# Split-weight blocks placed later, four more one-time slots for expert weights, in a fused transformer layer

## The chip, the cores and the metric

One core of a Trainium2 chip runs the whole layer as one program. The metric is the time of one execution on the device in microseconds (us). The engines named below are TensorE (PE; its weight loads are PEld), VectorE (DVE), ScalarE (ACT), GpSimd (POOL) and SyncE (SP), which here only issues transfers. Transfers are carried by 16 DMA engines shared by all queues.

## The reference

The layer takes 512 latent tokens and 256 context tokens of width 1024. It has two halves: token mixing (latent attention with 6 heads beside a Fourier mix of 256 channels, one output projection), and a mixture of 32 experts of which each token takes 4. The second half is the one that matters here:

```python
x = x + g1 * rms_norm(mix_x, norm_attn_post)           # after the output projection
hx2 = rms_norm(x, norm_ffn_pre) * (1 + sc2) + sh2
logits = hx2 @ w_router + b_router
top_logit, top_idx = lax.top_k(logits, 4)
gates = softmax(top_logit)
# for each expert e, over the tokens that chose it (xb):
g = minimum(xb @ w_gate[e] + b_gate[e], 7)
u = clip(xb @ w_up[e] + b_up[e], -7, 7)
y = (g * sigmoid(1.702 * g) * (u + 1)) @ w_down[e] + b_down[e]
# each token: the sum of its 4 y, weighted by its gates
x = x + g2 * rms_norm(moe, norm_ffn_post)
```

All is float32. Each of the 32 experts has three matrices of 1024 x 1024, 384 MiB in all, and every one of them has to be read.

## The kernel before

**The stages.** Up to about 335 us the kernel does the token mixing, ending with the output projection in four blocks of 128 tokens (`outp`). After each block follow `post(t)` (post-norm and residual on VectorE and ScalarE), `post_h(t)` (the token rows scaled by VectorE; for blocks 0 to 2 POOL adds the shift and stores the rows to `hx2_d` in DRAM; for block 3 VectorE adds), and `post_pe(t)` (router logits on PE, top 4 on VectorE). `pick(t)` gathers expert 0's tokens with matmuls. Then come the experts, to about 1335 us, and a short end with the last norm.

**The experts.** 32 units in a fixed order. Units 0 and 1 are experts 0 and 1, with 64 and 96 token slots; the others are chosen at run time by how many tokens came, and alternate: a larger one ("h", 128 slots, or "m", 96) and a smaller one ("l", 64, or "t", 32). Four are of kind "h"; their matmuls run on weights split into a high and a low part (`wsplit`: ScalarE writes the high part into `hi4`, VectorE the rest into `lo4`; four blocks of 4 KB per partition each, used in turn, 32 KB in all). The first "h" is unit 8, whose gate matrix is the 25th of 96 matrices (`order`).

**The weights.** A matrix comes in four pieces of 1 MiB (128 x 2 x 1024 float32), 384 pieces in the order of use. `load_piece(i)` issues piece i on SyncE's queue. Pieces 0 to NX - 1 go into one-time slots that are freed after use; the others share a ring of NRING = 11 slots. `emit_mat` computes one matrix; when it has used up piece p, it issues p + 11 if p is in the ring (p >= NX), otherwise it only frees the slot. `more_ring` takes the NX + NRING = 16 slots one after the other as memory of the first half comes free, and issues the piece that goes into each.

**A unit's tokens.** For each unit from 1 on, `gather` (inside `fetch_of`) computes row numbers, and POOL issues an indirect DMA (L1319) that reads the unit's token rows from `hx2_d`; `x_trans` transposes them on PE (the `tr` helper, L270) and copies them out of PSUM. `finish(ready.get(u))` puts all of that before the unit's first matmul.

**What sets the order.** Before the experts, a scheduler orders instructions by priority within what the data allow. From `manual_schedule` on (the expert phase) each engine runs in the order in which the code is written; `later` and `tick` delay single operations by a step. Memory is handed out by a list: PLAN holds one address per allocation, in the order of allocations. An allocation whose address overlaps an older block waits until that block's last use.

Helpers record most operations, so lines repeat: L266 matmul, L270 transpose, L274 ScalarE's activation, L278 two-input operation on VectorE or POOL, L289 VectorE's scalar-tensor-tensor, L978 the issue of a weight piece, L1144 and L1152 `post_h`'s product and shift.

Of the kernel before, what the change touches and what calls it, by code (L numbers as in the profile page):

```python
# [20 lines left out]
try:  # L21
# [6 lines left out]
F32R = mybir.dt.float32r  # L28
# [8 lines left out]
D = 1024  # L37
# [43 lines left out]
]  # L81


# [79 lines left out]
def dit_block(ctx: ExitStack, tc: tile.TileContext, x, c, cctx, c_ctx, w_mod, b_mod, n_ap, n_ao, n_fp, n_fo,  # L163
# [8 lines left out]
    vec_d = dr.tile([4, D], F32, name="vec_d")  # L172

    NRING = 11
    NX = 5
    WB = 5
    WT = 1
    WN = {2: 4, 3: 4, 4: 4, 5: 4}
    NB, LA = 4, 3
# [7 lines left out]
    def A(*dims, dt=F32, top=False):  # L187
        serial[0] += 1
        return T(nc, ar, f"s{serial[0]}", dims, dt, top)
# [14 lines left out]
    def alias(block, *dims, dt=F32):  # L204

        z = nc.alloc_sbuf_tensor_at(f"a{len(also)}", [128, *dims], dt, offset=block.o).ap()
        also[z.tensor.name] = block.t.tensor.name
        return z
# [48 lines left out]
    def free(*blocks):  # L257
        for z in blocks:
            n = z.t.tensor.name
            if any(n == q[0] for _, lo_, li_, _f in late for q in lo_ + li_):  # L260
                settle()
            z.free()
# [226 lines left out]
    for g in range(4):  # L489
        h = 64 * (g % 2)  # L490
# [454 lines left out]
    units = [("l", 0, None), ("m", 1, None)]  # L945
# [5 lines left out]
    order = [(0, "g"), (0, "u"), (1, "g"), (0, "d"), (1, "u"), (2, "g"), (1, "d")]  # L951
# [11 lines left out]
    def load_piece(i):  # L963
# [9 lines left out]
        else:  # L973
            src = wsrc[m][e:e + 1]
        slot = ring[i] if i < NX else ring[NX + (i - NX) % NRING]
        where[u, m, h] = slot
# [3 lines left out]
    def more_ring(n=None):  # L980
        while len(ring) < NRING + NX and (n is None or n > 0):
            ring.append(A(2, D))
            load_piece(len(ring) - 1)
            n = None if n is None else n - 1

    steps = [(u, m, k) for u, m in order for k in range(8)]

    def chunk(s):
        u, m, k = steps[s]
        return where[u, m, k // 2].f[:, k % 2]  # L990
# [191 lines left out]
    hi4, lo4 = [], []  # L1182

    def emit_split(s):
        if s < len(steps) and units[steps[s][0]][0] == "h":
            wsplit(s, chunk(s))

    def wsplit(s, z):
        hi, lo = hi4[s % NB].r, lo4[s % NB].r
        act(hi, z, AF.Copy)  # L1190
        later(lambda: tt(lo, z, hi, op=OP.subtract), [lo], [z, hi], age=0)

    for s in range(NB):
        hi4.append(A(D, dt=F32R))
        lo4.append(A(D, dt=F32R))
    for s in range(LA):
        emit_split(s)
    eid, eidi, selb = A(NS), A(NS, dt=I32), A(NS + 3, dt=BF)
    pm = CRp("pmod")
    V.memset(selb.b[:, NS + 2:NS + 3], 0.0)  # L1200
# [45 lines left out]
    kinds = [z[0] for z in units]  # L1246
# [198 lines left out]
    bank = {(0, "g"): 0, (0, "u"): 2, (1, "g"): 4, (0, "d"): 0, (1, "u"): 2, (2, "g"): 0, (1, "d"): 2}  # L1445
# [183 lines left out]
    def sel_of(u):  # L1629
        kind, e, r = units[u]  # L1630
        j = r if e is None else NS + e
        return selb.b[0:96, j:j + 1]
# [15 lines left out]
    def add(g, front=False):  # L1648
        z = Task(g)
        side.insert(0 if front else len(side), z)  # L1650
        return z
# [15 lines left out]
    def source(u, mat):  # L1667
        k = kinds[u]
        if mat == "d":
            return (aTh, aTl) if k == "h" else aTm if k == "m" else aT0 if u == 0 else aTf.f  # L1670
        return xT0 if k == "h" else (xT1.f if u == 1 else xTm) if k == "m" else xT64 if u == 0 else xTf.f
# [5 lines left out]
    def emit_mat(i, also=()):  # L1677
        also = list(also)
        for s in range(8 * i, 8 * i + 8):
            u, m, k = steps[s]  # L1680
            emit_split(s + LA)
            step_mm(kinds[u], m, bank[u, m], k, chunk(s), hi4[s % NB], lo4[s % NB], sel_of(u), source(u, m), u == 0)
            if k % 2:
                if s // 2 < NX:
                    free(ring[s // 2])
                elif s // 2 + NRING < len(pieces):
                    load_piece(s // 2 + NRING)
                else:
                    where[u, m, k // 2].free()
            side_step()  # L1690
            tick()
# [7 lines left out]
        yield  # L1699

    xT0 = (xTh, xTl)
    xTm = alias(xTh, 8, 128)
    ready, acted, summed = {}, {}, None
    add(routing())
    for i, (u, m) in enumerate(order):
        kind = kinds[u]
        if i:
            pu, was = order[i - 1]
            pk, pb = kinds[pu], bank[pu, was]
            if was == "g":  # L1710
                add(glu_g(pk, pb, pu == 0), True)
            elif was == "u":
                acted[pu] = add(chain(glu_u(pk, pb, {"h": 2, "m": 2, "l": 3, "t": 5}[kind] if pk == "h" else 0, pu == 0), a_trans(pk, pu == 0)), True)
            else:
                finish(summed)
                y_out(pu, pk, pb)
                if pu == 1:
                    summed = add(chain(chain_back(pu), rest(7), scatter(pu)))
                elif pu and pk in "lt":
                    summed = add(chain(chain_back(pu - 1), chain_back(pu), scatter(pu - 1, pu)))  # L1720
        if i == 5:
            summed = add(chain(bdown(), chain_back(0), scatter(0)))
        if i == 1:
            ready[1] = add(x_of(1))
        elif i == 2:
            add(fetch_of(2))
            add(fetch_of(0))
            add(fetch_of(3))
        elif i == 3:
            ready[2] = add(chain(x_of(2), fetch_of(4)))  # L1730
            add(chunk_plan())
        elif i == 6:
            ready[3] = add(chain(x_of(3), fetch_of(5)))
        elif m == "d" and u >= 2 and u + 2 < NU:
            x_ = x_of(u + 2)
            ready[u + 2] = add(chain(x_, fetch_of(u + 4)) if u + 4 < NU else x_)
        if (u, m) == (NU - 4, "g"):
            ntot, jcnt = W(1, dt=I32), W(1)
            cp(ntot.i, incl.f[:, NE - 1:NE])
            V.memset(jcnt.f, 0.0)  # L1740
            n_over = nc.values_load(ntot.i[0:1, 0:1], min_val=0, max_val=48, skip_runtime_bounds_check_because=SKIP)
        if m == "g":
            finish(ready.get(u))
        elif m == "d":
            finish(acted.get(u))
        if i + 1 == len(order):
            break
        emit_mat(i)
        if i == 0:
            settle()  # L1750
            t1, u1 = W(D), W(D)
            xT1 = W(8, 128)
        elif i == 1:
            while side:
                finish(side.pop(0))
            queued.close()
            free(lg, mask, maskb, Ub, onesb)
            aTh, aTl = R(8, 128), R(8, 128)
            aTm = alias(aTh, 8, 96)
            aT0 = alias(aTh, 8, 64)  # L1760
            yh, yl = R(D), R(D)
            acc = [W(D) for _ in range(4)]

            bdr = acc[3]
            for r in range(3):
                nc.sync.dma_start(bdr.f[32 * r:32 * r + 32], b_d)
        elif i == 4:
            settle()
            free(xT1)
            bd, gT, g3 = R(D), R(512), W(4, 96)  # L1770
            xTf = W(4, 128)
        elif i == 6:
            while side and side[0] is not ready[3]:
                finish(side.pop(0))
            settle()
            free(bd, g3, gT)
            aTf, u1l, yz = W(8, 64), W(512), R(D)
# [47 lines left out]
    for t in range(6):  # L1825
        if t < 4:
            for j in (2 * t, 2 * t + 1):
                both(j, j == 7, True)
            for j in (2 * t, 2 * t + 1):
                z = acc[t].f[:, 512 * (j % 2):512 * (j % 2) + 512]  # L1830
# [10 lines left out]
    with tc.For_i(0, n_over, 1):  # L1841
# [29 lines left out]
        for m in "gud":  # L1871
# [3 lines left out]
            for k in range(8):  # L1875
# [3 lines left out]
                z = slot.f[:, k % 2]  # L1879
# [37 lines left out]
```

## Time and profile before

| what | value |
|---|---|
| median of 3 runs | 1366.96 us (1366.21 to 1369.84) |
| the profiled execution, its own time | 1370.38 us |
| its span, first to last instruction | 1368.6 us |
| mean granted clock of TensorE | 0.986 |
| busy: PE, PEld | 1300.6 us (95%), 816.2 us (60%) |
| busy: VectorE, ScalarE, POOL | 740.0, 388.2, 119.3 us |
| moved by the DMA | 469.05 MB |

The profile is of one execution; its time is 1.8 us more than its span; differences are worked out from it and then carried to the median. Times in the trace count from the span's start. The busy share of an engine is a mean over the stages; which of two nearly full resources sets the end is to be read from who waits for whom.

### The profile page before, as it was taken

Reading aid. Unit: us, or ns where it says so; the run is one execution under the profiler, and the core shown is the slowest. Engines: PE = TensorE matmul, PEld = TensorE weight load, DVE = VectorE, ACT = ScalarE, POOL = GpSimd, SP = SyncE. Lnnn points to the kernel's source line nnn. Section 1 sums busy time; section 2 is a strip of 40 time slices with the busy share of each in tenths; the row PEclk is TensorE's granted clock in tenths of the full one; section 3 lists DMA queues with packets and bytes.
Section 4 is the critical chain, followed back from the end, with each engine's and each line's share of the span. In section 5 each row is a group of like instructions: output and inputs, shape, how many; then the busy total and the mean of one; then the engine's idle time right before and its main releaser. Section 6 shows DMA issues by size and latency. Waiting matters only on the chain. (4 is left out here: it accounts for less than half of the span.)

```text
span 1368.6 us, 33586 instructions
## 1 busy us (share of the span) xinstructions
PE 1300.6 (95%) x14518; PEld 816.2 (60%) x14518; DVE 740.0 (54%) x1393; ACT 388.2 (28%) x591; POOL 119.3 (9%) x89
## 2 busy tenths in 40 slices
PE   5999999999999999999999999999999999999993
PEld 3766888787455455566555555655555575555562
DVE  4676777756554334387343427752433477343675
ACT  5565444732111101054010103510110143010352
POOL 3355000003000000000000000000000000000002
PEclk8999999999999999999999999999999999999996
DMA  9876002749999999999999999999999999999993
GB/s 340 315 242 204 2 0 66 243 169 363 336 351 407 408 406 405 405 409 408 408 408 405 408 403 408 409 408 408 403 408 404 408 408 407 400 407 401 408 384 128
DMA packets 126507, 469.05 MB, mean 343 GB/s; under 512 B 10976, under 2 KB 12316, under 8 KB 126356
## 3 DMA queue, kind: packets, MB, share of 16 engines
q1 hardware_dynamic: 121540, 454.44, 84.9%
q0 software_dynamic: 4816, 12.43, 2.5%
q8 instruction: 115, 1.88, 0.6%
q14 instruction: 36, 0.29, 0.1%
HBM read 464.05 MB, written 6.31 MB: 344 GB/s over the span
## 5 line engine op out<-in xcount | busy, mean ns | idle before, releaser
L266 PE MATMUL ps<-s,s 128*32 128x256 f32 (+9 forms) x7307 | 874.0, 385 | 28.1 <-DVE s L278 10.0
L266 PEld LDWEIGHTS ps<-s,s 128*32 128x32 f32 (+3 forms) x6945 | 543.0, 139 | 297.2 <-issue 104.6
L266 PE MATMUL ps<-s,a 128*32 128x256 f32 (+1 forms) x6744 | 400.6, 384 | 0.0
L266 PEld LDWEIGHTS ps<-s,a 128*32 128x32 f32 x6744 | 212.2, 110 | 156.1 <-issue 20.6
L274 ACT ACTIVATE s<-s 128x1024 fp32r<-128x1024 f32 (+8 forms) x196 | 175.7, 926 | 388.6 <-DVE s L283 301.9
L278 DVE TENSOR_TENSOR s<-s,s 128x1024 fp32r<-128x1024 f32 (+11 forms) x316 | 207.9, 684 | 38.4 <-ACT s L274 34.7
L274 ACT ACTIVATE s<-ps 128x512 fp32r<-128x512 f32 (+5 forms) x151 | 82.6, 557 | 279.2 <-PE ps L266 139.2
L278 DVE TENSOR_TENSOR s<-s,ps 128x512 f32<-128x512 f32 (+1 forms) x129 | 86.2, 682 | 81.0 <-PE ps L266 80.5
L285 DVE TENSOR_SCALAR s<-ps 128x768 f32<-128x768 f32 (+3 forms) x32 | 26.1, 815 | 150.2 <-PE ps L266 150.2
L1319 POOL DMA_INDIRECT s<-hx_d,s x31 | 32.3, 1043 | 850.3 <-PE ps L266 577.6
L270 PE MATMUL ps<-s,s 128*128 128x128 f32 (+1 forms) x447 | 73.3, 286 | 18.0 <-DVE s L283 9.8
L293 DVE COPY s<-ps 128x4 f32<-128x4 f32 (+5 forms) x65 | 22.9, 358 | 123.3 <-PE ps L266 100.5
L270 PEld LDWEIGHTS ps<-s,s 128*128 128x128 f32 (+1 forms) x447 | 52.5, 144 | 54.0 <-issue 18.4
L289 DVE SCALAR_TENSOR_TENSOR s<-ps,s,s 64x512 fp32r<-64x512 f32 (+5 forms) x65 | 46.6, 718 | 54.9 <-ACT s L274 49.2
L274 ACT ACTIVATE s<-ps,s 64x512 fp32r<-64x512 f32 (+7 forms) x69 | 45.2, 665 | 93.5 <-PE ps L266 88.3
L297 DVE TENSOR_TENSOR s<-ps,s 128x512 fp32r<-128x512 f32 (+1 forms) x92 | 60.6, 667 | 19.1 <-ACT s L274 19.0
L283 DVE TENSOR_SCALAR s<-ps 128x768 f32<-128x768 f32 (+4 forms) x33 | 26.2, 795 | 75.4 <-PE ps L266 75.4
L278 POOL TENSOR_TENSOR s<-s,s 128x1024 f32<-128x1024 f32 (+1 forms) x19 | 43.3, 2288 | 251.6 <-DVE s L278 211.7
L274 ACT ACTIVATE a<-ps 128x512 f32<-128x512 f32 x22 | 13.1, 597 | 148.9 <-PE ps L270 148.8
L274 ACT ACTIVATE s<-s,s 128x1 f32<-128x1 f32 (+4 forms) x69 | 42.7, 646 | 13.2 <-DVE s L289 8.0
L297 DVE TENSOR_TENSOR s<-s,s 128x192 fp32r<-128x192 f32 (+5 forms) x32 | 36.0, 1144 | 8.8 <-ACT s L274 8.5
L289 DVE SCALAR_TENSOR_TENSOR s<-s,s,s 128x512 fp32r<-128x512 f32 (+5 forms) x47 | 36.4, 802 | 5.1 <-ACT s L274 4.6
(81 smaller groups left out, 327.5 us busy)
## 6 DMA issues: line engine op xcount, KB each, us to landing
s<-in_w_gate_dram SPq DMA_DIRECT2D x128, 1024.0 KB, 16.9
s<-in_w_up_dram SPq DMA_DIRECT2D x128, 1024.0 KB, 12.8
s<-in_w_down_dram SPq DMA_DIRECT2D x128, 1024.0 KB, 17.2
s<-in_w_mod_dram SPq DMA_DIRECT2D x32, 512.0 KB, 4.8
s<-in_w_mod_dram SPq DMA_DIRECT2D x8, 1024.0 KB, 13.5
s<-in_x_dram SPq DMA_DIRECT2D x8, 512.0 KB, 5.3
s<-in_w_out_dram SPq DMA_DIRECT2D x8, 512.0 KB
s<-in_w_in_dram SPq DMA_DIRECT2D x1, 2560.0 KB
```

Of the source, the lines that this page charges most:

```text
L266: pin(nc.tensor.matmul(o, a, b, start=start, stop=stop))
L270: pin(nc.tensor.transpose(o, i, ident))
L274: return nc.scalar.activation(o, i, f, **kw)
L278: return eng.tensor_tensor(o, a, b, op=op)
L283: eng.tensor_scalar(o, a, s1, s2, op0=op0)
L285: eng.tensor_scalar(o, a, s1, s2, op0=op0, op1=op1)
L289: V.scalar_tensor_tensor(o, a, s, b, op0=op0, op1=op1)
L293: eng.tensor_copy(o, i)
L297: later(lambda: eng.tensor_tensor(lo, src, hi, op=OP.subtract), [lo], [src, hi])
L1319: nc.gpsimd.indirect_dma_start(out=xg[kind], out_offset=None, in_=src, in_offset=bass.IndirectOffsetOnAxis(ap=idxs.i[:, u:u + 1], axis=0), ...
```

## The change

NX goes from 5 to 9: nine one-time slots, so 20 pieces instead of 16 have a place before the expert phase. The memory comes from the eight blocks `hi4` and `lo4`, which are no longer taken before the expert phase but right before the matrix ahead of the first "h" unit (while `emit_mat(23)` is about to run). Until then `emit_split` does nothing, and `step_mm` gets None in place of the blocks. PLAN has new addresses for nearly all allocations from there on, and the early ones of the expert phase with it. The ring keeps its 11 slots.

```diff
-    105120, 154272, 217088, 211456, 141984, 117408, 133792, 137888, 228288, 211328, 229088, 72096, 24736, 63776,
...
+    141984, 105120, 215552, 133792, 211456, 154272, 137888, 125600, 28896, 208416, 229088, 209728, 24736, 191264,
...
     NRING = 11
-    NX = 5
+    NX = 9
...
     def emit_split(s):
-        if s < len(steps) and units[steps[s][0]][0] == "h":
+        if s < len(steps) and units[steps[s][0]][0] == "h" and hi4:
             wsplit(s, chunk(s))
...
-    for s in range(NB):
-        hi4.append(A(D, dt=F32R))
-        lo4.append(A(D, dt=F32R))
-    for s in range(LA):
-        emit_split(s)
...
-            step_mm(kinds[u], m, bank[u, m], k, chunk(s), hi4[s % NB], lo4[s % NB], sel_of(u), source(u, m), u == 0)
+            step_mm(kinds[u], m, bank[u, m], k, chunk(s), *(z[s % NB] if z else None for z in (hi4, lo4)), sel_of(u), source(u, m), u == 0)
...
+    first_h = kinds.index("h")
...
+        if order[i + 1:i + 2] == [(first_h, "g")]:
+
+            for _ in range(NB):
+                hi4.append(A(D, dt=F32R))
+                lo4.append(A(D, dt=F32R))
         emit_mat(i)
```

SyncE's queue around the start of the expert phase stood so before (L1254 loads token numbers, L1766 expert biases; the w_down rows end expert 0, the w_up rows are expert 1's pieces 16 to 19; the last row reads an expert's number):

```order
L978 DMA s194_2585<-in_w_down_dram 128x2x1024
L978 DMA s208_2711<-in_w_down_dram 128x2x1024
L978 DMA s209_2713<-in_w_down_dram 128x2x1024
L978 DMA s212_2726<-in_w_down_dram 128x2x1024
L1254 DMA s222_2739<-in_tokens_dram 128x512
L978 DMA s181_2343<-in_w_up_dram 128x2x1024
L978 DMA s188_2537<-in_w_up_dram 128x2x1024
L978 DMA s189_2545<-in_w_up_dram 128x2x1024
L1766 DMA s250_2968<-in_b_down_dram 32x1024 x3
L978 DMA s190_2553<-in_w_up_dram 128x2x1024
L970 TENSOR_LOAD s204_2596
```

In the changed kernel the same stretch of the same queue is:

```order
L978 DMA s194_2585<-in_w_down_dram 128x2x1024
L978 DMA s200_2703<-in_w_down_dram 128x2x1024
L978 DMA s201_2705<-in_w_down_dram 128x2x1024
L978 DMA s204_2718<-in_w_down_dram 128x2x1024
L978 DMA s205_2720<-in_w_up_dram 128x2x1024
L978 DMA s206_2722<-in_w_up_dram 128x2x1024
L978 DMA s207_2724<-in_w_up_dram 128x2x1024
L978 DMA s208_2726<-in_w_up_dram 128x2x1024
L1249 DMA s218_2739<-in_tokens_dram 128x512
L1767 DMA s246_2965<-in_b_down_dram 32x1024 x3
L970 TENSOR_LOAD s196_2588
```

The four w_up pieces went into slots s181 and s188 to s190, used before; now they have slots of their own (s205 to s208) and stand directly behind the w_down pieces. Behind the last row both queues go on alike.

On VectorE the change shows in the last block of the output projection, between `post_pe(2)` (the first two rows) and `post(3)` (the last two); s161_2307 and s162_2308 are the token rows of blocks 0 and 1:

```order
 L289 SCALAR_TENSOR_TENSOR s176_2335<-ps_60,s186_2349 128x32
 L285 TENSOR_SCALAR s177_2336<-s158_2142,s176_2335,s170_2320 128x64
-L1144 SCALAR_TENSOR_TENSOR s207_2602<-s162_2308,s170_2320,s156_2136 128x1024
+L1144 SCALAR_TENSOR_TENSOR s199_2594<-s162_2308,s170_2320,s156_2136 128x1024
+L1144 SCALAR_TENSOR_TENSOR s198_2593<-s161_2307,s170_2320,s156_2136 128x1024
 L278 TENSOR_TENSOR s166_2312<-ps_60,s154_2134 128x512
 L285 TENSOR_SCALAR s170_2320<-s170_2320 128x1
```

Block 0's product stood one block earlier, before `post(2)`; it now stands behind block 1's, ahead of `post(3)`, since its output lies where the last output-projection weight (`woh[5]`) lay. POOL's add and store of block 0 move with it. From the first expert matmul on, the orders of PE, ScalarE and VectorE are the same in both.

## Rows read from the trace of the kernel before

**Rows 1.** The page: GB/s in 40 equal slices of the span (34.2 us each).

```profile
GB/s 340 315 242 204 2 0 66 243 169 363 336 351 407 408 406 405 405 409 408 408 408 405 408 403 408 409 408 408 403 408 404 408 408 407 400 407 401 408 384 128
```

**Rows 2.** Stretches: sum, busy PE, PEld, DVE, ACT, POOL (instructions), clock, DMA share, GB/s.

```profile
346.00:352.00 6.00, 4.81 (x76) 2.62 (x72) 3.24 (x11) 2.34 (x4) 0.00 (x0) 1.00 0.64 227
394.00:410.00 16.00, 16.00 (x209) 8.77 (x209) 8.98 (x17) 1.11 (x2) 0.00 (x0) 1.00 0.79 289
410.00:420.00 10.00, 10.00 (x188) 6.09 (x184) 3.12 (x10) 2.05 (x4) 1.00 (x1) 1.00 1.02 400
560.00:1320.00 760.00, 750.04 (x9215) 438.70 (x9211) 381.71 (x694) 166.65 (x223) 23.27 (x22) 1.00 1.03 407
```

**Rows 3.** Landing of weight pieces (L978) issued at 414:418, at 1085:1089, at 1317:1320.

```profile
DMA to landing us min/median/max: 6.2/7.0/7.8
DMA to landing us min/median/max: 20.0/20.1/20.2
DMA to landing us min/median/max: 18.7/19.4/20.1
```

**Rows 4.** PE's waits, 414 to 1320: total us, times, longest.

```profile
PE ps L266 <- DVE s L278: 8.9, 11, 1.8
...
```

**Rows 5.** ScalarE near the end: start, us, operation [idle before <-releaser].

```profile
1321.87 1.06 ACT L274 ACTIVATE s<-s 128x1024 fp32r<-128x1024 f32 x1 [8.27 <-DMA s<-in_w_down_dram]
```

**Rows 6.** SyncE's queue by time: start, us from first to last issue, operation, count.

```profile
347.54 6.49 SPq L978 DMA_DIRECT2D s<-in_w_up_dram  x3
...
356.58 0.39 SPq L978 DMA_DIRECT2D s<-in_w_up_dram  x1
...
394.24 23.38 SPq L978 DMA_DIRECT2D s<-in_w_up_dram  x8
```

**Rows 7.** PE's waits, 335 to 410, the whole answer.

```profile
PE ps L270 <- DMA s<-hx_d,s: 2.3, 2, 1.2
PE ps L270 <- DVE s L293: 0.6, 1, 0.6
```

**Rows 8.** PE by time: transposes of block 2, first expert matmuls, two gathers' transposes.

```profile
311.65 1.09 PE L270 MATMUL ps<-s,s 128*128 128x128 f32 x8 [0.77 <-DVE s L289]
...
335.69 6.25 PE L266 MATMUL ps<-s,a 128*32 128x256 f32 x112
...
348.66 0.63 PE L270 MATMUL ps<-s,s 128*128 128x128 f32 x4 [1.19 <-DMA s<-hx_d,s]
...
371.24 0.66 PE L270 MATMUL ps<-s,s 128*128 128x128 f32 x4 [1.15 <-DMA s<-hx_d,s]
```

**Rows 9.** Landing of gathers (L1319) issued at 340:350, 360:366, 410:420, 1086:1088.

```profile
DMA to landing us min/median/max: 4.5/4.5/4.5
DMA to landing us min/median/max: 8.8/8.8/8.8
DMA to landing us min/median/max: 5.1/5.1/5.1
DMA to landing us min/median/max: 7.4/7.4/7.4
```

**Rows 10.** POOL by time: two of its adds, and the gather of unit 1.

```profile
308.12 2.39 POOL L1152 TENSOR_TENSOR s<-s,s 128x1024 f32<-128x1024 f32 x1 [12.57 <-DVE s L1144]
...
320.53 2.35 POOL L1152 TENSOR_TENSOR s<-s,s 128x1024 f32<-128x1024 f32 x1 [7.87 <-DVE s L1144]
...
343.99 1.09 POOL L1319 DMA_INDIRECT s<-hx_d,s  x1 [4.41 <-issue]
```

**Rows 11.** VectorE by time, 306 to 324.

```profile
306.75 1.28 DVE L1144 SCALAR_TENSOR_TENSOR s<-s,s,s 128x1024 f32<-128x1024 f32 x1 [1.09 <-PE ps L266]
...
309.27 2.32 DVE L289 SCALAR_TENSOR_TENSOR s<-s,s,s 128x1024 f32<-128x1024 f32 x1
...
319.16 1.28 DVE L1144 SCALAR_TENSOR_TENSOR s<-s,s,s 128x1024 f32<-128x1024 f32 x1 [1.18 <-PE ps L266]
...
321.81 2.28 DVE L289 SCALAR_TENSOR_TENSOR s<-s,s,s 128x512 f32<-128x512 f32 x2
```

16 rows, old and new, of the table PLAN are left out of this document.

## The prediction

> **What bounds the kernel now.** I read four views in this order. The page first: of its 40 slices, the 13th (from 410 us) to the 38th all move 400 to 409 GB/s, those before it clearly less [rows 1].
>
> The table by stretch comes second. From 560 to 1320 us the DMA share is 1.03 at 407 GB/s and PE is busy 750.04 of 760 us, so both stand near their limit and no average tells which sets the end; from 410 to 420 the DMA is just as full (400 GB/s); but from 394 to 410 it carries only 289 GB/s while PE is busy all 16 us [rows 2]. So the saturated run begins at about 410 us.
>
> Third, who waits. From 414 to 1320 us the largest wait of PE is 8.9 us, for VectorE, and none of its rows names a weight transfer [rows 4]. What a loaded transfer shows instead is a growing queue: a weight piece issued at 414 to 418 lands after 7.0 us, at 1085 after 20.1, at 1317 after 19.4 [rows 3]. PE's releases thus come a little faster than the DMA can serve them, and only at the end is the eleven-piece cushion spent: ScalarE's split of the last 128-slot down-projection idles 8.27 us for a piece of w_down [rows 5]. The end is the start of the saturated run plus its bytes at 407 GB/s plus the tail. A change pays if it starts that run earlier, not if it takes a microsecond off PE after 420.
>
> Fourth, what starts the run. SyncE issues eight pieces over 23.38 us from 394.24 on [rows 6]: each goes out when PE has used up the piece eleven places before it, so in that stretch the DMA idles because PE has not yet freed a slot. PE's pace from its first expert matmul at 335.69 to about 410 is what starts the run, and from 335 to 410 nearly all that it waits for is two gathers of token rows, 2.3 us together, and no weights [rows 7]: 1.19 us before 348.66, 1.15 before 371.24 [rows 8].
>
> **The change part by part.**
>
> *Four more one-time slots.* Pieces 16 to 19 (expert 1's up-projection) lose their wait for the slots of pieces 5 to 8. Before, they are issued from 347.54 on, the last at 356.58 [rows 6]; now they have slots of their own, and they should go out at about 336, when the last attention blocks are freed. That is 4 x 1.049 MB / 407 GB/s = 10.3 us of transfer taken forward. But the ring is still eleven deep: piece 20 still follows the use of piece 9, and so on for all later ones. Since PE waits for no weights there [rows 7], these releases do not move, the DMA merely idles 10.3 us longer somewhere before 410, and the saturated run starts when it did. I cost this at 0. It needs the idle room of the stretch 394 to 410, where (407 - 289) / 407 x 16 = 4.6 us of transfer time lie empty before the full run; with that cover gone, the head start would be kept, as in the first rival.
>
> *Gather of expert 1, now beside full DMA.* POOL issues it at 343.99 [rows 10]; it lands in 4.5 us [rows 9], while the DMA moves 227 GB/s just after (346 to 352) [rows 2]. With pieces 16 to 19 in flight from 336 on, the pieces 12 to 19 keep the engines full until about 355, so this gather runs under load. Loaded gathers: 7.4 us at 1086, 8.8 at 360 to 366, 5.1 at 410 to 420 [rows 9]. PE already waits 1.19 us for it, so all that it grows is added to PE: 5.1 - 4.5 = +0.6 at least, 8.8 - 4.5 = +4.3 at most. I take the steady 7.4: +2.9. This shift lies ahead of 410, delays every release after it, and so the whole saturated run.
>
> The Trainium skill (DMA: Bandwidth & Descriptors, "Queues, rings and completion order") says that an engine takes turns between the queues that have work, a packet each. By that, a gather beside one full weight queue at most doubles, 4.5 to 9.0, and the sum below would be 4.5 - 2.9 = 1.6 us higher, an estimate; the trace agrees that a gather does not stand behind the whole backlog, since at 1086 it takes 7.4 us where weights take 20.1 [rows 3, 9].
>
> *Gather of expert 2.* It takes 8.8 us and costs PE 1.15 [rows 8, 9]. Now pieces 16 to 19 are out of its way, and only pieces 20 and on stand beside it. Anything at or under 7.4 takes the whole wait away (8.8 - 7.4 = 1.4, more than 1.15): -1.15, bounds 0 and -1.15.
>
> *Block 0's modulation moved.* hx[0] now lies where the last out-projection weight lay, so its multiply on VectorE, 1.28 us at 306.75 [rows 11], and POOL's add and store behind it, come after that of block 1, at the head of the last post-norm. Where it stood, it goes: at 309.27 an operation of the same shape takes 2.32 instead of 1.28 beside POOL's add (308.12, 2.39 us), and PE idles 0.77 before 311.65 for the line of that operation [rows 8, 10, 11]. Where it now stands, VectorE works from 319.16 on without a pause that could take it [rows 11], and the router of the last block hangs on it: +1.28. Net 1.28 - 0.77 = +0.5. POOL's adds slide too: now two stand in this chain. At 321.81 two operations of 128x512 take 2.28 us beside the add of 320.53 [rows 10, 11]. If POOL's add gets out of their way, about 1.1 us comes back (-0.6 in all); if the 0.77 isn't regained, +1.3. I take +0.5.
>
> *The rest.* The eight split blocks are placed before piece 92 is used instead of before the expert phase; no instruction is in that. The two engine orders from 336 on are the same on PE, ScalarE and VectorE. SyncE issues pieces 16 to 19 ahead of the small loads of token numbers and b_down; these are needed many us later: 0.
>
> Sum, against the profiled execution: 1370.38 + 0.5 + 2.9 - 1.15 = 1372.6. That execution is 3.4 us over the median of the runs shown, 1366.96, so the median of the changed kernel should be 1366.96 + 2.25 = 1369.2. Its own range, from the bounds: -0.6 + 0.6 - 1.15 = -1.15 to 1.3 + 4.3 - 0 = +5.6, 1365.8 to 1372.6.
>
> **Rivals.**
>
> *The head start is kept (faster).* If the DMA were in truth the limit from 336 on, 10.3 us of transfer moved forward would end the run 10.3 us sooner: 1366.96 - 10.3 = 1356.7. For it: the end waits for transfers [rows 5]. Against: 289 GB/s at 394 to 410 [rows 2], releases by PE [rows 6], and no wait of PE for weights before 410 [rows 7]. 0.09.
>
> *Gather 1 isn't slowed.* If weights and gather share the engines so that its few rows pass, only the second wait goes: 0.5 - 1.15 = -0.65, 1366.3. For it: 5.1 us at 410 to 420 under 400 GB/s [rows 2, 9]. Against: 7.4 and 8.8 elsewhere. 0.19.
>
> *Block 0's work lands whole in the last chain (slower).* VectorE's 1.28 and POOL's add of 2.35, which holds back VectorE's operations with two inputs as at 309.27 and 321.81 [rows 10, 11], both before the router, with nothing regained: 3.6 + 2.9 - 1.15 = +5.4, 1372.3. It decides if the first expert matmul, now at 335.69 [rows 8], starts at 339 or later. For it: VectorE has no pause there. Against: the 0.77 that goes, and VectorE's first operation may get ahead of POOL's add. 0.17.
>
> The Trainium skill (SBUF — State Buffer, "Who interferes with whom") has a rule that speaks for this rival: an operation of VectorE with two inputs in SBUF contends with a GpSimd instruction that reads SBUF, and whichever comes second is held back wholly. The 2.32 against 1.28 agrees.
>
> **How the numbers follow.** The forecast has 0.55, the rivals 0.09, 0.19 and 0.17. A measurement of this kernel tells a difference of about 0.3%, 4.1 us: "same" is 1362.9 to 1371.1. Of the forecast 0.07 lies above that (gather at 8.8 with the upper bound of the moved work), 0.48 in it; the second rival lies in it whole, of the third 0.02; the first is faster, with 0.01 more for a mixture. Faster 0.10, same 0.68, slower 0.22. The range: down to 1364.0, the second rival with its lower bounds (-0.6 - 1.15 = -1.75, 1365.2) and some 1.2 for the runs, of which the fastest lies 0.75 under the median; up to 1373.0, the third rival and 0.7 of the same. That leaves out the first rival and a few hundredths above.
>
> **What would show it.** In the changed trace: SyncE issues of w_up at about 336 instead of 347.5 (the head start); a hole in the DMA at about 355 to 360, and 394 to 410 again under 300 GB/s; weight pieces at 1317 again landing after 19 to 20 us; the gather issued at about 344.5 landing after 7 us, with PE waiting about 4 us for it; no wait at the second gather; the first expert matmul at about 336.2. The prediction is wrong if the saturated run starts more than 3 us earlier than 410, or if the queue at 1317 is clearly shorter with the last split's wait gone.

## The result, and the profile after

The changed kernel takes 1378.74 us (median of 6 runs, 1376.22 to 1381.25), the kernel before 1368.51 beside it (6 runs); the ratio is 1.0060, 95% interval 1.0041 to 1.0078. The medians themselves differ by 10.2 us (0.75%); the ratios here and below are those on record, which are not quotients of the two medians. Forecast were 1369.2, within 1364.0 to 1373.0: the time lies above the range, and the change is slower by 0.6%, not the same. The profiled execution took 1380.88 us with a span of 1379.1, so it is 10.5 us longer than the profiled one of before.

PE by time (start, us, operation, idle before it and what ended it), the changed kernel (the first line shown are the transposes of block 1, ahead of all that follows here):

```profile
297.95 0.60 PE L270 MATMUL ps<-s,s 128*128 128x128 f32 x4
...
322.89 0.66 PE L270 MATMUL ps<-s,s 128*128 128x128 f32 x4 [1.18 <-DVE s L289]
326.12 0.66 PE L270 MATMUL ps<-s,s 128*128 128x128 f32 x4 [2.57 <-DVE s L289]
326.61 9.49 PE L266 MATMUL ps<-s,s 128*128 128x64 f32 x48
...
342.03 6.25 PE L266 MATMUL ps<-s,a 128*32 128x256 f32 x112
...
360.62 1.12 PE L270 MATMUL ps<-s,s 128*128 128x128 f32 x4 [6.82 <-DMA s<-hx_d,s]
...
367.42 8.95 PE L266 MATMUL ps<-s,s 96*32 96x512 bf16 x156
```

The same view of the kernel before, the lines of it that were not shown:

```profile
298.50 0.60 PE L270 MATMUL ps<-s,s 128*128 128x128 f32 x4
...
324.64 5.47 PE L266 MATMUL ps<-s,s 128*128 128x64 f32 x48
...
353.42 11.55 PE L266 MATMUL ps<-s,s 96*32 96x512 bf16 x204
```

The first expert matmul starts 6.3 us later (335.69 in [rows 8]), and the transposes of unit 1's tokens wait 6.82 us for their gather instead of 1.19. The 0.77 us at 311.65 and the wait at the second gather are gone. Start times of two profiles hold an offset from earlier stages: block 1's transposes stand at 298.50 before and at 297.95 here, and in a second profile of the same changed kernel (c_after_again below) at 295.86. Counted from these transposes the first expert matmul comes after 37.2 us before and 44.1 us here, 6.9 later. Behind the wait for the gather, the work up to the next line shown takes 6.8 us (360.62 to 367.42) where it took 4.8 (348.66 to 353.42). The 48 matmuls behind the last block's transposes take 9.49 us instead of 5.47; the table by stretch says why (sum, busy PE, PEld, DVE, ACT, POOL, then clock, DMA share, GB/s):

```profile
328.00:336.00 8.00, 8.00 (x38) 8.00 (x40) 3.79 (x10) 0.00 (x0) 3.81 (x2) 0.50 1.02 410
354.00:358.00 4.00, 0.00 (x0) 0.00 (x0) 1.74 (x3) 0.00 (x0) 0.00 (x0) 1.00 1.01 286
358.00:374.00 16.00, 13.38 (x196) 7.35 (x200) 4.55 (x14) 1.20 (x2) 0.00 (x0) 0.79 0.06 14
410.00:420.00 10.00, 10.00 (x124) 5.29 (x127) 6.42 (x14) 0.82 (x2) 0.00 (x0) 1.00 0.67 229
560.00:1320.00 760.00, 750.90 (x9394) 438.52 (x9385) 373.25 (x686) 161.86 (x219) 23.29 (x22) 1.00 1.02 408
```

Behind each of the two idle stretches of PE the granted clock is at the lower of its two levels (0.50, which is 1.2 GHz, from 328 to 336; 0.79 as a mean of 358 to 374). In the kernel before it is 1.00 in every stretch shown [rows 2], and in the one of the 48 matmuls too:

```profile
328.00:336.00 8.00, 7.31 (x62) 5.32 (x65) 5.62 (x14) 0.81 (x2) 4.04 (x3) 1.00 0.90 357
```

And the DMA moves 14 GB/s from 358 to 374: the head start was spent in idling, as forecast. The lightly loaded stretch that lay at 394 to 410 lies behind 410 now (229 GB/s from 410 to 420). From 560 on both kernels run alike.

VectorE by time, in the changed kernel, at the place to which block 0's work moved:

```profile
317.59 2.48 DVE L1144 SCALAR_TENSOR_TENSOR s<-s,s,s 128x1024 f32<-128x1024 f32 x2 [1.86 <-PE ps L266]
...
321.44 4.62 DVE L289 SCALAR_TENSOR_TENSOR s<-s,s,s 128x512 f32<-128x512 f32 x2
```

POOL by time around it, up to the gather of unit 1:

```profile
318.96 3.32 POOL L1152 TENSOR_TENSOR s<-s,s 128x1024 f32<-128x1024 f32 x1 [0.33 <-DVE s L1144]
...
323.15 2.35 POOL L1152 TENSOR_TENSOR s<-s,s 128x1024 f32<-128x1024 f32 x1
...
341.24 0.52 POOL L1261 MEMSET s<- 128x512 f32 x1 [8.03 <-DMA hx_d<-s]
341.74 0.55 POOL L1155 DMA_DIRECT2D hx_d<-s  x1
350.77 1.09 POOL L1314 DMA_INDIRECT s<-hx_d,s  x1 [8.48 <-DVE s L278]
```

VectorE's pair of operations takes 4.62 us against 2.28 [rows 11]; the 2.34 more are the length of POOL's add of block 0 (2.35), which stands between them. PE waits for exactly these (2.57 at 326.12). The rule of the Trainium skill (SBUF — State Buffer, "Who interferes with whom") that the later of the two is held back wholly agrees with that.

The last three lines were not foreseen. The store of block 3's rows stands on POOL behind a memset of a gather buffer, and that memset waits until a store of hx_d has landed, since the buffer now lies where block 2's rows lay. The gather needs all four stores. In this profile the order costs little: VectorE's add of block 3 ends at 340.10, 1.6 us ahead of the store, and the gather goes out 8.7 us behind the first expert matmul, where it was 8.3 before (343.99 behind 335.69). What grew is its landing. Landing of the store issued at 341.74:

```profile
DMA to landing us min/median/max: 8.2/8.2/8.2
```

Landing of the gather issued at 350.77:

```profile
DMA to landing us min/median/max: 9.8/9.8/9.8
```

The gather took 4.5 before [rows 9]; block 3's store, issued at 334.29 in the kernel before, took 3.8:

```profile
DMA to landing us min/median/max: 3.8/3.8/3.8
```

SyncE's queue shows the head start (pieces 16 to 19 at 341, forecast at about 336) and that later releases moved with PE: the eight pieces issued from 394.24 on [rows 6] are 12.8 us later.

```profile
341.10 2.30 SPq L978 DMA_DIRECT2D s<-in_w_up_dram  x4
...
407.05 23.33 SPq L978 DMA_DIRECT2D s<-in_w_up_dram  x8
```

### The profile page after: what moved, and what is told of

It is laid out like the page before. It is cut to its first block, busy times and chain, and to the rows that moved or that the text cites. A ratio compares the mean times of both kernels' runs of the same rounds, so it can differ in the third digit from the quotient of the medians.

```text
span 1379.1 us, 33583 instructions
## 1 busy us (share of the span) xinstructions
PE 1306.9 (95%) x14516; PEld 822.0 (60%) x14518; DVE 739.6 (54%) x1393; ACT 388.2 (28%) x591; POOL 120.3 (9%) x89
## 5 line engine op out<-in xcount | busy, mean ns | idle before, releaser
L274 ACT ACTIVATE s<-s,s 128x1 f32<-128x1 f32 (+4 forms) x69 | 42.7, 647 | 12.7 <-DVE s L289 8.0
```

The source lines that it names most:

```text
L274: return nc.scalar.activation(o, i, f, **kw)
```

## The experiments

Twelve runs were made in three groups (the first four rows, the next four, the last four), each on one chip beside the kernel before; ratios of different groups come from different chips. Added lines shift the line numbers of the views a little. Two expectations call the gather's landing in the changed kernel 10.5 us; that was misread, it is the 9.8 above.

| run | edit, on the changed kernel | median us (n) | before beside it | ratio, 95% interval |
|---|---|---|---|---|
| e1_hx0_place | block 0's rows elsewhere | 1374.42 (12) | 1369.53 | 1.0038, 1.0023 to 1.0052 |
| e2_late_pieces | pieces 16 to 19 written later in the code | 1378.35 (6) | 1369.53 | 1.0060, 1.0038 to 1.0083 |
| e3_both_undone | both of these | 1375.09 (12) | 1369.53 | 1.0041, 1.0029 to 1.0054 |
| e5_keep_clock | PE kept busy in its wait | 1378.10 (6) | 1369.53 | 1.0060, 1.0037 to 1.0083 |
| e6_store_order | e1 and store ahead of memset | 1370.23 (12) | 1370.65 | 1.0011, 0.9995 to 1.0027 |
| e7_late_13_19 | e6 and pieces 13 to 19 held back | 1366.63 (12) | 1370.65 | 0.9975, 0.9964 to 0.9986 |
| e8_late_16_19 | e6 and pieces 16 to 19 held back | 1366.29 (12) | 1370.65 | 0.9968, 0.9951 to 0.9985 |
| e9_deeper_ring | e7 and three more ring slots at first | 1367.62 (12) | 1370.65 | 0.9989, 0.9972 to 1.0007 |
| c_after_again | none | 1379.67 (6) | 1370.45 | 1.0077, 1.0057 to 1.0097 |
| e5b_keep_clock | as e5 | 1376.98 (6) | 1370.45 | 1.0055, 1.0035 to 1.0075 |
| e10_store_order_only | store ahead of memset | 1380.00 (6) | 1370.45 | 1.0072, 1.0050 to 1.0094 |
| e11_late_16_19_only | pieces 16 to 19 held back | 1376.56 (12) | 1370.45 | 1.0037, 1.0019 to 1.0055 |

**e1_hx0_place.** The address of hx[0] alone:

```diff
-... 227264, 227392, 227680, 129696, 150176, ...
+... 227264, 227392, 227680, 221696, 150176, ...
```

> The changed kernel with one address altered: block 0's token rows (hx[0]) lie where no out-projection weight is still in use, so that VectorE's product and POOL's add of block 0 stand again before post(2). The four early pieces 16 to 19 stay early. Theory 1 (two separate causes: the moved add of POOL holds up VectorE and with it PE, whose clock then falls, +6.3 us up to the first expert matmul; and the gather of unit 1 beside full DMA, another 6 to 7 us): first expert matmul back at 335.7 +- 0.7 us instead of 342.0, no stretch at half clock before it, the gather still landing after 8 to 10.5 us with PE waiting 4 to 7 us; median 1371 to 1374, about 6 us under the changed kernel. Theory 2 (the early pieces alone do it, by loading the DMA; the moved add is harmless): no change, 1378 to 1379. Theory 3 (other new addresses are at fault): first expert matmul stays near 342.

PE by time in e1:

```profile
295.60 0.60 PE L270 MATMUL ps<-s,s 128*128 128x128 f32 x4
...
334.30 6.25 PE L266 MATMUL ps<-s,a 128*32 128x256 f32 x112
...
353.72 1.12 PE L270 MATMUL ps<-s,s 128*128 128x128 f32 x4 [7.65 <-DMA s<-hx_d,s]
```

The first expert matmul came at 334.30, 38.7 us behind block 1's transposes, against 44.1 in the changed kernel and 37.2 before: block 0's place explains 5.4 of the 6.9 us, part of them through the clock (looked at below). The other 1.5 us are as much as the 48 matmuls lose to a lower clock that stayed: they take 6.93 us instead of 5.47. The median fell by 0.2% in ratio, a little less than expected; PE now waits longer for the gather (7.65 us). POOL's lines show that the store of block 3 still stood behind the memset, though its add had begun at 330.91 and takes 1.22:

```profile
335.03 0.52 POOL L1261 MEMSET s<- 128x512 f32 x1 [7.08 <-DVE a L1226]
335.54 0.54 POOL L1155 DMA_DIRECT2D hx_d<-s  x1
344.99 1.10 POOL L1314 DMA_INDIRECT s<-hx_d,s  x1 [8.90 <-DVE s L1380]
```

Theory 2 fell. Of theory 1 the first half holds, but for its clock; the second half, a gather late only by full DMA, was incomplete: here, where block 3's add ends at 332.13, the memset holds its store until 335.54, and the gather goes out 10.7 us behind the first expert matmul.

**e2_late_pieces, e3_both_undone.** The same edit of the loading, on the changed kernel and on e1:

```diff
             ring.append(A(2, D))
-            load_piece(len(ring) - 1)
+            if len(ring) <= 16:
+                load_piece(len(ring) - 1)
...
                     free(ring[s // 2])
+                    if s // 2 >= 5:
+                        load_piece(s // 2 + NRING)
```

> The changed kernel, with pieces 16 to 19 in their own slots but issued only when PE has used up pieces 5 to 8, as in the kernel before; block 0's work stays moved. Theory 1: first expert matmul still near 342.0, the gather of unit 1 lands after 4.5 to 5 us and PE waits 1 to 1.7 us for it, the second gather costs about 1.2 again; PE is then some 6.3 us behind the kernel before and the median is 1373 to 1375. Theory 2 (early pieces alone): 1368.5, as before. If the head start were worth anything, this kernel would lose more than the changed one, over 1379.

> Both edits together: block 0's rows at a free address and pieces 16 to 19 issued as late as before, on the changed kernel's memory (nine one-time slots, split blocks taken late). Theory 1: the whole loss is gone, 1368.5 +- 2, first expert matmul at 335.7, gather of unit 1 landing after 4.5 us. Theory 3 (some other part of the change, as the new addresses or the late split blocks, costs too): over 1371.

Both missed: 1.0060 and 1.0041, no change against their bases. The edit did not do what was meant. Its place in the code puts a piece behind PE's step only if something makes SyncE wait, and a slot that nobody used makes it wait for nothing. In e3 pieces 16 to 18 go out from 332.71 on, before PE's first expert matmul at 333.64. So these two say nothing on the head start; what they showed is PE's wait in e3, 9.96 us, with the memset and store in the order above.

```profile
332.71 1.92 SPq L978 DMA_DIRECT2D s<-in_w_up_dram  x3
```

**e5_keep_clock, e5b_keep_clock, c_after_again.** One number altered, `keep_busy(8)` to `keep_busy(24)` (so many matmuls on a block of zeros); the last is the changed kernel itself.

> The changed kernel with 24 instead of 8 matmuls on a block of zeros ahead of the last block's transposes, so that PE is busy in the 3.7 us in which it waits for VectorE; nothing else is altered. Theory 1 (of the 6.3 us before the first expert matmul some 4 are a clock at half after that idle time): granted clock 1.00 from 318 to 342, the 48 matmuls of 64 columns behind the transposes take 5.5 us instead of 9.5, first expert matmul at about 338; median 4 us under the changed kernel, 1374 to 1375.5. Rival (the clock follows something else than PE's idle time, or VectorE's chain sets the first expert matmul anyway): first expert matmul stays at 341 to 342, no gain.

> The kernel of e5_keep_clock again, beside the changed kernel on one chip: its profiled execution was 4 us shorter than that of the changed kernel, its median only 0.6 us. If the half clock ahead of the first expert matmul occurs in every execution of the changed kernel: 3 to 5 us under c_after_again. If only in some: under 2 us, and the profile of c_after_again may show the 48 matmuls of 64 columns at 5.5 us.

> The changed kernel once more, on the chip of the next three runs, to compare them with: 1377 to 1380, first expert matmul at 341 to 343, PE waits 6 to 7.5 us for the gather of unit 1, half clock at about 328 to 336 and again at 358 to 365.

The profile agrees in part: first expert matmul at 337.54 and 337.90 instead of 342.03 and 343.82 (behind block 1's transposes 41.3 and 42.7 us instead of 44.1 and 48.0). The clock was not wholly kept, though: from 318 to 342 its mean is 0.79 in the changed kernel, 0.64 in c_after_again, 0.93 in e5 and 0.86 in e5b. The medians fell by 0.6 us in the one pair (two chips, the ratios are alike; 4 us were expected) and by 2.7 in the other, and the intervals overlap: what this edit is worth at the end was not settled, between 0 and 3 us. The executions of single kernels say that the clock's level goes with more than that. Of e11's twelve, three took 1369.5 to 1370.8 us at a mean granted clock of 0.984 to 0.986, and nine 1375.6 to 1380.7 at 0.979 to 0.981; of e9's twelve, nine took 1364.4 to 1369.1 at 0.984 to 0.990, and three 1371.2 to 1375.7 at 0.980 and 0.981. No run parts the clock from the waits that come with it, so what is cause in this is not shown. Nor is the cause of the lower clock settled, and theory 1 on it fell in part: in e1 PE waits only 0.21 us ahead of the 48 matmuls, and the clock is down all the same.

PE by time in e1, the transposes and the 48 matmuls:

```profile
319.65 1.32 PE L270 MATMUL ps<-s,s 128*128 128x128 f32 x8 [0.21 <-DVE s L289]
320.81 6.93 PE L266 MATMUL ps<-s,s 128*128 128x64 f32 x48
```

The stretch in which they end, in e1 (columns as above):

```profile
328.00:336.00 8.00, 7.71 (x67) 4.48 (x69) 2.67 (x6) 1.38 (x4) 0.97 (x2) 0.79 1.03 417
```

c_after_again also shows how the two losses trade. Its half-clock stretch was longer (first expert matmul at 343.82), and PE's wait for the gather shorter, 3.06 us instead of 6.82 (6 to 7.5 were expected): the gather landed at 359.4 in this profile (7.1 us behind its issue) and at 360.6 in the first.

```profile
359.41 1.12 PE L270 MATMUL ps<-s,s 128*128 128x128 f32 x4 [3.06 <-DMA s<-hx_d,s]
```

**e6_store_order.** On e1:

```diff
-        nc.gpsimd.dma_start(hx2_d[t * 128:t * 128 + 128], h)
+        stored.append(nc.gpsimd.dma_start(hx2_d[t * 128:t * 128 + 128], h))
...
-        nc.gpsimd.memset(z.f, 0.0)
+        with tc.issue_after(stored[-1].ins):
+            nc.gpsimd.memset(z.f, 0.0)
```

> The changed kernel with block 0's rows at a free address (as in the run e1_hx0_place), and POOL's two memsets of the gather buffers kept behind the store of block 3 in POOL's order, as they stood in the kernel before. Theory A (the gather of unit 1 is late because the store of block 3's rows waits on POOL behind a memset whose buffer now lies over block 2's rows, and because stores and gather run beside weight pieces): the store of block 3 is issued some 3 us earlier than in e1_hx0_place, within 0.5 us of its last add; PE waits 4 to 6 us for the gather instead of 7.65; median 1371 to 1373.5, some 2 us under e1_hx0_place. Theory B (the store's place does not matter; only full DMA makes the gather late): wait 7 to 8 us as before the edit, 1374.4.

Theory A holds, with a median a little lower than expected. The store goes out at 332.32, the gather at 342.01, 8.3 us behind the first expert matmul (333.72) instead of e1's 10.7; PE waits 4.18 instead of 7.65. Ratio 1.0011, where e1 has 1.0038 on another chip, and the two intervals just overlap: with block 0's place and this order undone, the loss is gone within the interval.

```profile
332.32 0.54 POOL L1157 DMA_DIRECT2D hx_d<-s  x1 [3.38 <-issue]
332.85 0.97 POOL L1264 MEMSET s<- 128x1024 f32 x1
336.29 0.52 POOL L1264 MEMSET s<- 128x512 f32 x1 [2.47 <-DMA hx_d<-s]
342.01 1.09 POOL L1317 DMA_INDIRECT s<-hx_d,s  x1 [5.20 <-DVE s L293]
```

PE by time in e6:

```profile
349.67 0.63 PE L270 MATMUL ps<-s,s 128*128 128x128 f32 x4 [4.18 <-DMA s<-hx_d,s]
```

**e7_late_13_19, e8_late_16_19.** On e6, a column of the slot is written by VectorE ahead of the load, so that SyncE has to wait (e8 has the second part alone):

```diff
+            if 14 <= len(ring) <= 16:
+                with tc.issue_after(shifted[-1].ins):
+                    V.memset(ring[-1].f[:, 0, 0:1], 0.0)
...
+                    if s // 2 >= 5:
+                        V.memset(ring[s // 2 + NRING].f[:, 0, 0:1], 0.0)
+                        load_piece(s // 2 + NRING)
```

> As e6_store_order, and pieces 13 to 19 are held back by a memset of one column of their slots on VectorE: 13 to 15 until VectorE has added the shift to block 3, 16 to 19 until the steps at which PE uses up pieces 5 to 8 are reached. With that nothing of the change is left but the memory's layout, and the DMA is as lightly loaded around the stores and the gather as before. Theory A: store lands in about 4 us, gather in 4.5 to 5.5, PE waits 0.5 to 2 us for it; first expert matmul at 333.7 to 335; median 1366 to 1369, no slower than the kernel before. Theory C (something else in the layout or the late blocks costs): over 1371.

> As e7_late_13_19, but only pieces 16 to 19 are held back; 13 to 15 go out when memory is free, some 10 us earlier than in the kernel before. Tells which of the early pieces load the DMA at the gather. If 16 to 19 alone do it: as e7, wait 0.5 to 2 us, 1366 to 1369. If the earlier 13 to 15 do it (they delay the store of block 3): wait 3 to 6 us, 1370 to 1373.

Both as theory A has it, and alike: so 16 to 19 do it, and the earlier 13 to 15 cost nothing. In e8 the gather lands in 4.5 us, PE waits 1.21 us for it, and 1.10 for the second, as before the change:

```profile
334.37 6.25 PE L266 MATMUL ps<-s,a 128*32 128x256 f32 x112
...
347.35 0.63 PE L270 MATMUL ps<-s,s 128*128 128x128 f32 x4 [1.21 <-DMA s<-hx_d,s]
...
369.88 0.66 PE L270 MATMUL ps<-s,s 128*128 128x128 f32 x4 [1.10 <-DMA s<-hx_d,s]
```

From e6 to e8 is another 0.4%, the price of the early pieces. Whether the store's order still matters once these pieces are late was not run. Both kernels beat the one before (0.9968 and 0.9975). Their first expert matmuls start 1.3 and 1.0 us earlier, but in e8 that lead is there already at block 1's transposes (297.04, the offset named above), and only e7 is faster from there on (36.2 us against 37.2; e8 37.3). Near the end both wait less for weights, as the changed kernel does (shown below). Neither was tried by itself, so why they are faster than the kernel before stays open.

**e9_deeper_ring.** On e7, the slots of pieces 6 to 8 join the ring until the split blocks need them, and some addresses of the last stage move with the ring's phase:

```diff
-        slot = ring[i] if i < NX else ring[NX + (i - NX) % NRING]
+        slot = ring[i if i < 20 else 6 + (i - 6) % 14 if i < 90 else 9 + (i - 79) % 11]
...
+                new = [p + 14] if p < 76 else [p + 11]
```

> As e7_late_13_19, and the slots of pieces 6 to 8, which the changed kernel leaves empty until the split blocks take them, serve as three more slots of the ring until then: piece p + 14 instead of p + 11 follows the use of p, up to p = 75; then p + 11 as before. The head start of the change is thereby kept by the ring. Theory: the DMA has no hole between 394 and 410, pieces are up to 7.7 us ahead, the waits for weights near the end (some 3 us of PE, 8.3 us of ScalarE at 1322 in the kernel before) go: 2 to 4 us under e7_late_13_19, 1363 to 1366. Rival (PE sets the time all along, the DMA is early enough): as e7.

The rival holds. The hole at 394 to 410 is filled (409 GB/s where the kernel before has 289 [rows 2]), the head start is kept, and the time is not lower: 0.9989, against 0.9975 for e7. PE waits 2.53 us for the second gather, beside the fuller DMA, instead of 1.03 in e7; that wait hides no gain, since from the second gather's transposes to the end both profiles take 994.9 us.

```profile
394.00:410.00 16.00, 16.00 (x213) 8.75 (x216) 8.99 (x17) 1.12 (x2) 0.00 (x0) 1.00 1.03 409
```

PE by time in e9:

```profile
370.85 0.66 PE L271 MATMUL ps<-s,s 128*128 128x128 f32 x4 [2.53 <-DMA s<-hx_d,s]
```

**e10_store_order_only, e11_late_16_19_only.** The edits of e6 and e8, each alone on the changed kernel.

> The changed kernel with POOL's two memsets of the gather buffers behind the store of block 3, nothing else: block 0's work stays in the last chain, the early pieces stay early. The store can go out 1.5 us earlier (its add ends at 340.2, it was issued at 341.74), no more, since here block 3 itself is late; PE waits 5 to 6 us for the gather instead of 6.8; 1 to 2 us under c_after_again. If the memset's place were worth its 4 us here too, it would be 4 under.

> The changed kernel with pieces 16 to 19 held back on VectorE as in e8_late_16_19, nothing else: block 0's work stays in the last chain, the memset stays ahead of the store of block 3. Theory: the store lands in 4 to 5 us instead of 8.5, the gather in 4.5 to 5.5 instead of 10.5, PE waits 1 to 2 us for it (6.8), and the clock does not fall behind that wait; first expert matmul still at 342; 6 to 8 us under c_after_again, 1370.5 to 1373. Rival (the memset ahead of the store decides by itself): PE still waits 4 us or more, 1374 to 1376.

e10 gained nothing (1380.00 beside 1379.67): with block 0's work in the chain, block 3 is late itself and the memset hides behind it; the order is worth its 0.3% only once that is undone. e11 gained 3.1 us, half of what was expected. The wait fell to 0.33 us and the gather landed in 4.3, as the theory has it:

```profile
355.95 0.66 PE L270 MATMUL ps<-s,s 128*128 128x128 f32 x4 [0.33 <-DMA s<-hx_d,s]
```

But the sum was made from the wait of 6.82 in the first profile, and beside it the changed kernel waited 3.06. Three of e11's executions, those at the higher mean clock, do lie in the forecast 1370.5 to 1373 or under it; the profile is of one of the other nine.

## Why the prediction was wrong

*The head start, 0: held.* The DMA idles from 358 to 374, and releases from piece 20 on follow PE. e9 goes further: a head start that is kept is worth nothing either.

*What sets the end: wrong reading, without effect on the sum.* The idle 8.27 us of ScalarE [rows 5] were taken for a DMA limit. PE itself lost 1.5 us there (0.42 for ScalarE and 1.06 for VectorE, which write the split weights), and e9 shows that filling the DMA earlier gains nothing. PE's delay before 410 is what counts: 12.8 us in SyncE's releases, of which the span shows 10.5. PE by time near the end, before and then in the changed kernel:

```profile
1320.80 0.66 PE L270 MATMUL ps<-s,s 128*128 128x128 f32 x4
...
1330.09 14.27 PE L266 MATMUL ps<-s,s 128*128 128x512 f32 x107 [1.06 <-DVE s L278]
```

```profile
1332.98 0.66 PE L270 MATMUL ps<-s,s 128*128 128x128 f32 x4
...
1340.64 14.20 PE L266 MATMUL ps<-s,s 128*128 128x512 f32 x107 [0.45 <-DVE s L278]
```

The delay is 12.2 us at the first of these lines and 10.55 at the second, so most of the difference lies between them, where the changed kernel waits less for split weights.

*Block 0's modulation moved, +0.5 with -0.6 to +1.3: the step that failed first.* It measured +6.9 us, counted from block 1's transposes (+6.3 by start times). The third rival had the mechanism, POOL's add holding back VectorE; it got 0.17, and its sign, a first expert matmul at 339 or later, came. Two things made the step too small. First, about what was taken to come back did so (VectorE's product of block 1 starts 1.0 us earlier, counted from those transposes), but the last chain paid for the product (+1.2) and for the add (+2.3) in full: PE waited 1.18 and 2.57 us there, where the kernel before has 0.21, and its 48 matmuls start 2.5 us later. That is under the rival's +3.6 too. Second, the clock was in no term, of the forecast or of the rival: the 48 matmuls behind those waits run mostly at the lower level, +4.0 us in the profile (e1: +1.5, without the waits). e1 undoes 5.4 of the 6.9 us.

*Gather of unit 1, +2.9 with +0.6 to +4.3: right sign and mechanism, too small.* PE's wait grew by 5.6 us in the profile, 5.3 of it by the landing, 9.8 us where 7.4 was taken and 8.8 was the bound. The early pieces make it so: with them held back, the changed kernel's gather lands in 4.3 us (e11), e8's in 4.5. Over all runs with early pieces the landing was 6.0 to 9.8 us. The estimate that the prediction worked out from the Trainium skill (DMA: Bandwidth & Descriptors, "Queues, rings and completion order"), at most 9.0 us, was nearer to 9.8 than the 7.4 that was taken, and the landing went past it. Two things had no term. Behind the longer wait the clock fell again, and the next work took 2.0 us more (6.8 against 4.8). And the store of block 3, on which the gather depends, moved behind a memset on POOL, because the buffer of that memset now lies over block 2's rows: in the changed kernel that delays the gather by no more than 0.4 us (8.7 behind the first expert matmul against 8.3), and e10 gains nothing; it is worth 0.3% once block 0's work is out of the way (e6).

*Gather of unit 2, -1.15: held.* No wait is left there in the changed kernel; in e9 it grew to 2.53. So 6.9, 5.6 and 2.0, less 1.15 and the offset of 0.55, make the 12.8 us of SyncE's releases.

## What to carry to other kernels

When an allocation changes its address, look at every instruction that waits for the old tenant, and then at what stands behind it on its engine: here a memset of 0.5 us held a store (by 3.4 us in e1), and an add of 2.35 us an operation of VectorE for its whole length. A transfer brought forward where the engine that consumes it does not wait for it gains nothing and takes bandwidth from small transfers on which it does wait. A place in the code is no time for a DMA queue: into a fresh slot a piece goes out when the queue comes to it (in e3, ahead of the step of PE behind which it was written).

## What was not expected of the hardware

Waits of PE of 1.18 and 2.57 us, 3.2 us apart, were followed by the lower clock in both profiles of the changed kernel (mean from 328 to 336: 0.50); a wait of 6.82 us was followed by it again. But waits are not all: in e1 the mean of that stretch was 0.79 with 0.21 us of waiting ahead of it, and with 16 more matmuls on zeros (e5, e5b) it was 0.79 and 0.58. In the kernel before the same work, with waits of up to 1.19 us, ran at 1.00. Over all profiles the waits and the depth of the fall go together: the mean of that stretch was 0.50 in all five with the waits of 1.18 and about 2.57 us, and 0.79 to 1.00 in the seven with 0.21 (1.00 in e7 and in the kernel before). What decides among those seven was not found.
